# A two-layer hybrid decoder trunk: the last key tile in the ring of the others, memory banks read by halves together, and alternating rings for the second layer's key weights

## The chip and the metric

The kernel runs on one core of a Trainium2 chip. Its engines are named as the profile names them: PE (the matmul engine; PEld is its weight load), ACT, DVE, POOL and SP, which here only issues loads. The metric is the device time of one execution in microseconds (us), smaller being better; the median of three runs is given.

## The reference, cut to what matters

```python
mem_n = rmsnorm(mem, norm_mem)                    # 256 memory tokens
for layer in range(2):
    h = rmsnorm(x, norm_mix[layer])
    if layer == 0:                                # 8 heads x 64, strictly causal, and pooling
        q, k, v, u = split(h @ ab_w_in)
        mix = concat(stick_breaking_attention(q, k, v), multiscale_pool(u)) @ ab_w_out
    else:                                         # 64 groups of 16 channels, 64 complex states
        y = s5_ssm(h @ ssm_w_in)
        val, gate = split(gelu(y) @ ssm_w_glu)
        mix = val * sigmoid(gate)
    x = x + mix
    k, v = split(mem_n @ w_kv[layer])             # the keys and values of the memory
    x = x + cross_attention(rmsnorm(x, norm_xattn[layer]) @ w_q, k, v) @ w_o
    x = x + conv_gated_mlp(rmsnorm(x, norm_ffn[layer]))
return rmsnorm(x, norm_final)
```

There are 512 positions of 1024 channels, in fp32.

## The kernel before

Activations lie with channels on partitions, in tiles of 128 x 512. A product of two fp32 matrices is made of three matmuls on a high and a low part of each side (`mm3`, L206 to L209: high by high, high by low, low by high). The high part is a rounded copy made by ACT (`copy_hi`, L113), the low part the difference, made by DVE (`sub_lo`, L116).

Weights come as chunks of 128 x 512 through one stream, `W`. A chunk is loaded by SP into a raw buffer `wr`, and then split by ACT and DVE into a high and a low tile. A chunk of kind 0 goes to `wh` and `wl`, of which four pairs may wait ahead; one of kind 1 goes to `wth` and `wtl`, which are taken from the common ring of tiles `t` (`ttile`), and of those two pairs may wait ahead in the second layer. `W.take` hands PE the next chunk in the fixed order of the list and puts the splits of further chunks behind what ACT and DVE have been given so far. A chunk that is split late frees its raw buffer late, and SP waits for raw buffers.

Instructions run on each engine in the order in which the program is written: the two mixing stages are lists of small steps (`seq`), and each step gives each engine its part.

In the first layer's stage the steps of a head h are `z_(h)` (scores, PE `psz` at L1096 to L1103, then ACT and DVE), `f_(h)` (the running sums, PE at L1136, then the weights `swh` and `swl` by ACT and DVE) and `p_(h)` (weights times values, PE `pso`, split into `mh` and `ml`). `q_(p)` and `k_(p)` make the query and key tile of two heads: PE `psqk`, DVE `qkf`, then a split into `qk`. The tiles of pairs 0 to 2 lie in a ring `qk` of six buffers; those of pair 3 lie in the buffers `vh0` and `vh1` of the pool `kv0`, the home of the memory's values later on. The earlier tenant of `vh1` is `par`, parameters of the state-space stage; its last reader is PE's `psmu`.

Memory tokens enter by `acts(q)`: PE transposes two column blocks into one PSUM bank `psm` (L217), ACT writes the high part of each half (`mem`, L778), DVE the low part (L779). The banks of `psm`, `pso` and `psz` come from one rotation; the three banks of `z_(5)` are those that `acts(2)`, `p_(3)` and `acts(3)` have left, in this order (with the change `acts(2)`, `acts(3)`, `p_(3)`). `kk(m)` is PE's product of the memory with two key columns (`psk`), four chunks of 128 x 512.

In the second layer's stage the memory is transposed and scaled anew (`ac(q)`), between the steps of the state-space part. For a block b these are `um(b)` (PE `psu`, the input projection), `uo` and `sg` (out to DRAM and back in another layout, tile `sg`), `x1(b)` (PE `psX`; ACT `xs` and `mub`; DVE `sr`, `xs`, `sr` and the scan into `gg`), `x2(b)` (ACT `gsw`; DVE `gg`, `gsw` and `hb`) and `x3(b)` (PE `psY`, which needs `sg` and `hb`; ACT `sy`). `hb` is read from `psY`'s second matmul on (L1703).

Of the kernel before, what the change touches and what calls it, by code (L numbers as in the profile page):

```python
# [8 lines left out]
F32 = mybir.dt.float32  # L9
F32R = mybir.dt.float32r  # L10
I32 = mybir.dt.int32
BF16 = mybir.dt.bfloat16
AF = mybir.ActivationFunctionType
ALU = mybir.AluOpType
# [8 lines left out]
MEM = 256  # L23
# [29 lines left out]
def trunk_kernel(  # L53
# [12 lines left out]
    V, A, G, T = nc.vector, nc.scalar, nc.gpsimd, nc.tensor  # L66
# [28 lines left out]
    def psB(name="psB"):  # L95
        if "X" in pools:
            return psX(name)
        return pools["B"].tile([128, 512], F32, tag="ps", name=name)

    def psC(name="psC"):  # L100
        if "X" in pools:
            return psX(name)
        return pools["C"].tile([128, 512], F32, tag="ps", name=name)

    def ttile(name, dt=F32R):
        return tp.tile([128, 512], dt, tag="t", name=name)
# [5 lines left out]
    def copy_hi(o, i):  # L112
        A.activation(out=o, in_=i, func=AF.Copy)  # L113

    def sub_lo(o, i, hi):
        V.tensor_tensor(out=o, in0=i, in1=hi.bitcast(F32), op=ALU.subtract)  # L116
# [80 lines left out]
    def sproj(ps, acts, n=512, first=True, last=True):  # L197
        k, nk = 0, len(acts)
        while k < nk:
            hi, lo = W.take()  # L200
            for q in range(hi.shape[1]):
                mm3(ps, hi[:, q, :], lo[:, q, :], acts[k][0][:, :n], acts[k][1][:, :n],
                    first and k == 0, last and k == nk - 1)
                k += 1
# [11 lines left out]
    def tr(o, i, kk=128):  # L216
        T.transpose(o, i, ident[:kk, :kk])  # L217
# [14 lines left out]
    def gcol(idx, layer, m):  # L232
        c = goff[idx] + layer * KD + m
        return gcols[:, c:c + 1]
# [36 lines left out]
    def norm_row(rc, n, perm=False, dst=None, dg=None):  # L271
        if dg is None:
            dg = norm_diag(rc, n)
        pr = psC("psrow")
        T.matmul(pr[:, :n * 128], lhsT=ones, rhs=dg[:, :n, :], start=True, stop=True)
        if dst is None:
            dst = np_.tile([128, 512], F32, tag="rbc", bufs=1, name="rbc")
        if perm:
            A.activation(out=dst.rearrange("p (j k) -> p j k", j=8),
                         in_=pr.rearrange("p (k j) -> p j k", j=8), func=AF.Copy)  # L280
        else:
            A.activation(out=dst[:, :n * 128], in_=pr[:, :n * 128], func=AF.Copy)
        return dst
# [445 lines left out]
    class KV:  # L729
# [35 lines left out]
        def acts(self, m0=0, m1=KD):  # L765
            if m0 == 0:
                self.ma = []
            for m in range(m0, m1, 2):
                ps = psC("psm")
                for q in range(2):  # L770
                    for i in range(2):
                        tr(ps[:, q * MEM + i * 128:q * MEM + (i + 1) * 128],
                           self.mr[i][:, (m + q) * 128:(m + q + 1) * 128])
                for q in range(2):
                    t = ttile("mem")
                    h, l = t[:, 0:MEM], t[:, MEM:2 * MEM]
                    g, p = gcol(3, 0, m + q), ps[:, q * MEM:(q + 1) * MEM]
                    A.activation(out=h, in_=p, func=AF.Copy, scale=g)  # L778
                    V.scalar_tensor_tensor(out=l, in0=p, scalar=g, in1=h.bitcast(F32), op0=ALU.mult, op1=ALU.subtract)  # L779
                    self.ma.append((h, l))  # L780
            if m1 < KD:
                return
            self.kh = self.pool.tile([128, KD, MEM], F32R, tag="kh", name="kh")
            self.kl = self.pool.tile([128, KD, MEM], F32R, tag="kl", name="kl")
# [48 lines left out]
    def glu_col(i):  # L833
        return (i + 1) % 2 * KD + i // 2

    def ssm_weights():
        kw = KV.weights(1)
        for b in range(NB):
            W.cols(ssm_w_in[0], b)
            if b >= 4:  # L840
                W.todo += kw[4 * (b - 4):4 * (b - 3)]
        W.todo += kw[16:]
        for i in range(NG1):
            W.cols(ssm_w_glu[0], glu_col(i), 0, 6)
        for i in range(NG1):
            W.cols(ssm_w_glu[0], glu_col(i), 6, 2)
        for i in range(NG1, 2 * KD):
            W.cols(ssm_w_glu[0], glu_col(i))
# [22 lines left out]
    kv0 = tc.alloc_tile_pool(name="kv0", bufs=1, reuse_waits="tile")  # L871
# [16 lines left out]
    for q in ("kh", "kl"):  # L888
        t = kv0.tile([128, 2048], F32, tag=q, name="par")
        par += [t[:, c * 512:(c + 1) * 512] for c in range(4)]  # L890
    for q in ("vh0", "vh1"):
        t = kv0.tile([128, 1024], F32, tag=q, name="par")
# [148 lines left out]
    with region("rgA1") as rg, tc.manual_schedule():  # L1041

        def rt(tag, bufs, name, dt=F32):
            return rg.tile([128, 512], dt, tag=tag, bufs=bufs, name=name)

        vh, vl = [], []
        for i in range(4):
            h = rt("v", 8, "vh", F32R)
            l = rt("v", 8, "vl", F32R)
            A.activation(out=h, in_=pv[i], func=AF.Copy, scale=rcol0[:, i:i + 1])  # L1050
            V.scalar_tensor_tensor(out=l, in0=pv[i], scalar=rcol0[:, i:i + 1], in1=h.bitcast(F32),
                                   op0=ALU.mult, op1=ALU.subtract)
# [5 lines left out]
        def qk_tile(name, scale):  # L1058
            ps = psB("psqk")
            sproj(ps, n_mix0.acts)  # L1060
            if not rbc0:
                rbc0.append(norm_row(None, 4, dg=dg0))
            f = np_.tile([128, 512], F32, tag="ev", bufs=2, name="qkf")
            V.scalar_tensor_tensor(out=f, in0=ps, scalar=scale, in1=rbc0[0], op0=ALU.mult, op1=ALU.mult)
            if name[1] == 3:
                t = kv0.tile([128, 1024], F32R, tag="vh0" if name[0] == "q" else "vh1", name="qk3")
                h, l = t[:, 0:512], t[:, 512:1024]
            else:
                h, l = rt("qk", 6, "qkh", F32R), rt("qk", 6, "qkl", F32R)
            copy_hi(h, f)  # L1070
            sub_lo(l, f, h)
            qk[name] = (h, l)
# [140 lines left out]
        def seq(*fs):  # L1213
            for f in fs:
                if type(f) is int:
                    step(f)
                else:
                    f()
# [10 lines left out]
        q_ = lambda p: (lambda: qk_tile(("q", p), 0.125))  # L1229
        sq = lambda q: (lambda: kvm.square(q))  # L1230
        k_ = lambda p: (lambda: qk_tile(("k", p), 1.0))
        z_ = lambda h: (lambda: sb_z(h))
        f_ = lambda h: (lambda: sb_f(h))
        p_ = lambda h: (lambda: sb_p(h))
        u_ = lambda g: (lambda: pool_in(g))
        ud = lambda g: (lambda: pool_sum(g))
        uf = lambda g: (lambda: pool_fin(g))
        um = lambda g: (lambda: pool_mm(g))
        kk = lambda m: (lambda: kvm.k(m))
        acts = lambda q: (lambda: kvm.acts(2 * q, 2 * q + 2))  # L1240
# [2 lines left out]
        seq(f_(0), z_(1), k_(1), p_(0), 1, 1)  # L1243
        seq(f_(1), ud(2), z_(2), um(3), q_(2), uf(2), 1, p_(1), u_(1), um(2))
        seq(f_(2), kvm.stats, ud(1), z_(3), 1, u_(0), 1, uf(1), kvm.row, k_(2), 1, 1, 1, turn_on, p_(2))
        seq(f_(3), 1, um(1), 1, ud(0), 1, 1, q_(3), 1, z_(4), 1, 1, acts(0), acts(1), k_(3), 1, acts(2), p_(3), acts(3))
        seq(f_(4), fin, uf(0), z_(5), kk(0), p_(4), um(0), kk(1))
        seq(f_(5), z_(6), kk(2), p_(5), kk(3), v_(0))
        seq(f_(6), z_(7), v_(1), p_(6))
# [1 line left out]
        for m in range(KD):  # L1251
            ps = ab_out(m)
# [599 lines left out]
```

## Time and profile before

| | us |
|---|---|
| median of three runs | 1499.33 (1497.9 to 1500.23) |
| the profiled execution, its time | 1498.06 |
| its span, first to last instruction | 1496.3 |
| PE busy | 1477.7 (99%) |
| DVE busy | 1028.7 (69%) |
| ACT busy | 735.1 (49%) |
| POOL busy | 395.3 (26%) |

Page rows give the share of the whole span. The chain of work that ended last runs through PE for 92% of the span, DVE for 3%, ACT for 2%. The mean granted clock of PE is 0.994 of full speed. In a row of the trace in order of time, the bracket at the end gives how long the engine had been idle and what it had waited for; an operation with "x16" is a run of sixteen.

### The profile page before, as it was taken

Reading aid. Unit: us, or ns where it says so; the run is one execution under the profiler, and the core shown is the slowest. Engines: PE = TensorE matmul, PEld = TensorE weight load, DVE = VectorE, ACT = ScalarE, POOL = GpSimd, SP = SyncE. Lnnn points to the kernel's source line nnn. Section 1 sums busy time; section 2 is a strip of 40 time slices with the busy share of each in tenths; the row PEclk is TensorE's granted clock in tenths of the full one; section 3 lists DMA queues with packets and bytes.
Section 4 is the critical chain, followed back from the end, with each engine's and each line's share of the span. In section 5 each row is a group of like instructions: output and inputs, shape, how many; then the busy total and the mean of one; then the engine's idle time right before and its main releaser. Section 6 shows DMA issues by size and latency. Waiting matters only on the chain.

```text
span 1496.3 us, 21038 instructions
## 1 busy us (share of the span) xinstructions
PE 1477.7 (99%) x7347; PEld 1234.8 (83%) x7347; DVE 1028.7 (69%) x1607; ACT 735.1 (49%) x1304; POOL 395.3 (26%) x823
## 2 busy tenths in 40 slices
PE   8999999999999999999999999999999999999998
PEld 7887888888888887888788898888888888888887
DVE  4776776676688897888865766556567775377755
ACT  5566774344445534555664555434444543245533
POOL 7864119999000013333852120000000000000002
PEclk9999999999999999999999999999999999999999
DMA  6313243433433344444568985332233333333331
GB/s 183 98 46 102 67 151 100 119 94 104 129 99 107 113 147 147 123 123 132 158 189 302 269 269 182 106 97 67 60 94 89 97 97 97 100 95 99 97 115 57
DMA packets 271941, 183.99 MB, mean 123 GB/s; under 512 B 21271, under 2 KB 252763, under 8 KB 271835
## 3 DMA queue, kind: packets, MB, share of 16 engines
q1 hardware_dynamic: 244731, 132.79, 30.3%
q0 software_dynamic: 15872, 42.26, 8.5%
q10 hardware_dynamic: 11232, 7.61, 1.6%
q8 instruction: 57, 0.93, 0.3%
q14 instruction: 49, 0.40, 0.1%
HBM read 156.13 MB, written 24.12 MB: 120 GB/s over the span
## 4 chain that ended last, share of the span: by engine, by line
PE 92%; DVE 3%; ACT 2%; DMA 1%; issue 1%; SPq 0%; ACTq 0%; DVEq 0%; POOLq 0%; POOL 0%
PE psup L207 10%; PE psup L209 10%; PE psup L208 10%; PE psd L207 5%; PE psd L209 5%; PE psd L208 5%; PE pso L209 2%; PE pso L208 2%; PE pso L207 2%; PE psq L207 2%; PE psq L209 2%; PE psq L208 2%; PE psg L207 2%; PE psg L209 2%; PE psg L208 2%; PE psz L1136 1%
## 5 line engine op out<-in xcount | busy, mean ns | idle before, releaser
L116 DVE TENSOR_TENSOR wl<-wr,wh 128x512 fp32r<-128x512 f32 (+2 forms) x467 | 325.1, 713 | 143.9 <-ACT wh L113 142.8
L113 ACT ACTIVATE wh<-wr 128x512 fp32r<-128x512 f32 (+2 forms) x467 | 280.1, 617 | 249.5 <-PE psup L208 83.3
L207 PE MATMUL psup<-xh,wh 128*128 128x512 f32 x704 | 275.7, 392 | 0.0
L208 PE MATMUL psup<-xl,wh 128*128 128x512 f32 x704 | 274.4, 390 | 0.0
L209 PE MATMUL psup<-xh,wl 128*128 128x512 f32 x704 | 274.1, 389 | 0.0
L1542 POOL TENSOR_TENSOR acc<-acc,sq 128x256 f32<-128x256 f32 x12 | 8.8, 734 | 557.2 <-ACT sq L1540 557.0
L207 PEld LDWEIGHTS psup<-xh,wh 128*128 128x128 f32 x704 | 132.2, 188 | 28.5 <-issue 1.5
L209 PEld LDWEIGHTS psup<-xh,wl 128*128 128x128 f32 x704 | 132.2, 188 | 28.3 <-DVE wl L116 0.3
L208 PEld LDWEIGHTS psup<-xl,wh 128*128 128x128 f32 x704 | 132.2, 188 | 27.1 <-issue 0.2
L207 PE MATMUL psd<-hh,wh 128*128 128x512 f32 x328 | 130.5, 398 | 0.0
L209 PE MATMUL psd<-hh,wl 128*128 128x512 f32 x328 | 128.3, 391 | 0.0
L208 PE MATMUL psd<-hl,wh 128*128 128x512 f32 x328 | 127.9, 390 | 0.2 <-DVE hl L116 0.2
L1456 ACT ACTIVATE fc<-fu,ccols 128x512 f32<-128x512 f32 x44 | 36.0, 817 | 93.6 <-DVE fu L1454 93.6
L302 ACT ACTIVATE xh<-xT,gcols 128x512 fp32r<-128x512 f32 x40 | 33.4, 835 | 95.2 <-DVE xT L325 66.8
L207 PEld LDWEIGHTS psd<-hh,wh 128*128 128x128 f32 x328 | 61.6, 188 | 14.4 <-issue 1.5
L209 PEld LDWEIGHTS psd<-hh,wl 128*128 128x128 f32 x328 | 61.6, 188 | 13.6
L208 PEld LDWEIGHTS psd<-hl,wh 128*128 128x128 f32 x328 | 61.7, 188 | 13.0 <-DVE hl L116 0.5
L715 POOL DMA_DIRECT2D tz<-kt x128 | 65.1, 516 | 7.4 <-POOL kt L712 4.7
L303 DVE SCALAR_TENSOR_TENSOR xl<-xT,gcols,xh 128x512 fp32r<-128x512 f32 x40 | 35.2, 880 | 33.7 <-ACT xh L302 33.5
L207 PE MATMUL psq<-xh,wh 128*128 128x512 f32 x128 | 51.1, 400 | 0.0
L1401 DVE TENSOR_TENSOR fu<-psup,rbc 128x512 f32<-128x512 f32 x44 | 30.3, 688 | 29.2 <-PE psup L209 27.9
L207 PE MATMUL pso<-oh,wh 128*128 128x512 f32 x128 | 50.2, 392 | 0.0
(352 smaller groups left out, 3441.2 us busy)
## 6 DMA issues: line engine op xcount, KB each, us to landing
wr<-in_ffn_w_up_dram SPq DMA_DIRECT2D x176, 256.0 KB, 3.0
wr<-in_ffn_w_down_dram SPq DMA_DIRECT2D x70, 256.0 KB, 2.9
wr<-in_xa_w_kv_dram SPq DMA_DIRECT2D x64, 256.0 KB, 4.1
wr<-in_ab_w_in_dram SPq DMA_DIRECT2D x32, 256.0 KB, 2.8
wr<-in_xa_w_q_dram SPq DMA_DIRECT2D x32, 256.0 KB, 2.9
wr<-in_xa_w_o_dram SPq DMA_DIRECT2D x32, 256.0 KB, 2.8
wr<-in_ssm_w_glu_dram SPq DMA_DIRECT2D x29, 256.0 KB, 2.8
wr<-in_ffn_w_down_dram SPq DMA_DIRECT2D x24, 192.0 KB, 2.6
```

The costliest lines, as they stand in the source:

```text
L113: A.activation(out=o, in_=i, func=AF.Copy)
L116: V.tensor_tensor(out=o, in0=i, in1=hi.bitcast(F32), op=ALU.subtract)
L207: T.matmul(ps, lhsT=lh, rhs=rh, start=first, stop=False)
L208: T.matmul(ps, lhsT=lh, rhs=rl, start=False, stop=False)
L209: T.matmul(ps, lhsT=ll, rhs=rh, start=False, stop=last)
L302: A.activation(out=ho, in_=src, func=AF.Copy, scale=g)
L303: V.scalar_tensor_tensor(out=lo, in0=src, scalar=g, in1=ho.bitcast(F32), op0=ALU.mult, op1=ALU.subtract)
L715: nc.gpsimd.dma_start(out=tzs[b % 2][j:128:8, :, j * 16:128], in_=ktf[:, :, 0:128 - j * 16])
L1136: T.matmul(o_, lhsT=l_, rhs=r_, start=False, stop=(n_ == len(mms) - 1), skip_group_check=True)
L1401: V.tensor_tensor(out=u, in0=ps, in1=rbc, op=ALU.mult)
L1456: A.activation(out=c, in_=u, func=AF.Identity, scale=cwcol(layer, 2, t), bias=cbcol(layer, t))
L1542: G.tensor_tensor(out=acc[:, sl], in0=acc[:, sl], in1=sq[:, 0:256], op=ALU.add)
```

## The change

Four places in the code change.

- `KV.acts`: of a bank of two halves, ACT now reads both, and then DVE both. Before, the order was ACT, DVE, ACT, DVE, and each had to wait for the one ahead, since they read the same bank.
- `KV.weights(1, (0, 1))`: of the second layer's key chunks every second one is of kind 1, in the common ring (`wth`, `wtl`). The first layer has that already.
- `qk_tile`: the key tile of pair 3 takes the next two buffers of the ring `qk`, those of key tile 1, in place of `vh1`. The query tile of pair 3 stays in `vh0`.
- The list of the first layer: `acts(3)` stands ahead of `p_(3)`.

```diff
@@ -774,10 +774,12 @@
                 for q in range(2):
                     t = ttile("mem")
                     h, l = t[:, 0:MEM], t[:, MEM:2 * MEM]
-                    g, p = gcol(3, 0, m + q), ps[:, q * MEM:(q + 1) * MEM]
-                    A.activation(out=h, in_=p, func=AF.Copy, scale=g)
-                    V.scalar_tensor_tensor(out=l, in0=p, scalar=g, in1=h.bitcast(F32), op0=ALU.mult, op1=ALU.subtract)
+                    A.activation(out=h, in_=ps[:, q * MEM:(q + 1) * MEM], func=AF.Copy, scale=gcol(3, 0, m + q))
                     self.ma.append((h, l))
+                for q in range(2):
+                    h, l = self.ma[m + q]
+                    V.scalar_tensor_tensor(out=l, in0=ps[:, q * MEM:(q + 1) * MEM], scalar=gcol(3, 0, m + q),
+                                           in1=h.bitcast(F32), op0=ALU.mult, op1=ALU.subtract)
             if m1 < KD:
                 return
             self.kh = self.pool.tile([128, KD, MEM], F32R, tag="kh", name="kh")
@@ -834,7 +836,7 @@
         return (i + 1) % 2 * KD + i // 2
 
     def ssm_weights():
-        kw = KV.weights(1)
+        kw = KV.weights(1, (0, 1))
         for b in range(NB):
             W.cols(ssm_w_in[0], b)
             if b >= 4:
@@ -1062,8 +1064,8 @@
                 rbc0.append(norm_row(None, 4, dg=dg0))
             f = np_.tile([128, 512], F32, tag="ev", bufs=2, name="qkf")
             V.scalar_tensor_tensor(out=f, in0=ps, scalar=scale, in1=rbc0[0], op0=ALU.mult, op1=ALU.mult)
-            if name[1] == 3:
-                t = kv0.tile([128, 1024], F32R, tag="vh0" if name[0] == "q" else "vh1", name="qk3")
+            if name == ("q", 3):
+                t = kv0.tile([128, 1024], F32R, tag="vh0", name="qk3")
                 h, l = t[:, 0:512], t[:, 512:1024]
             else:
                 h, l = rt("qk", 6, "qkh", F32R), rt("qk", 6, "qkl", F32R)
@@ -1243,7 +1245,7 @@
         seq(f_(0), z_(1), k_(1), p_(0), 1, 1)
         seq(f_(1), ud(2), z_(2), um(3), q_(2), uf(2), 1, p_(1), u_(1), um(2))
         seq(f_(2), kvm.stats, ud(1), z_(3), 1, u_(0), 1, uf(1), kvm.row, k_(2), 1, 1, 1, turn_on, p_(2))
-        seq(f_(3), 1, um(1), 1, ud(0), 1, 1, q_(3), 1, z_(4), 1, 1, acts(0), acts(1), k_(3), 1, acts(2), p_(3), acts(3))
+        seq(f_(3), 1, um(1), 1, ud(0), 1, 1, q_(3), 1, z_(4), 1, 1, acts(0), acts(1), k_(3), 1, acts(2), acts(3), p_(3))
         seq(f_(4), fin, uf(0), z_(5), kk(0), p_(4), um(0), kk(1))
         seq(f_(5), z_(6), kk(2), p_(5), kk(3), v_(0))
         seq(f_(6), z_(7), v_(1), p_(6))
```

First place: ACT in the first layer, behind the weight splits, up to the scores' exponential. The names carry tile numbers; `psm` is the bank of one `acts`, `mh` the split of `pso`, and a bracket lists the engines that the instruction waits for. Before:

```order
L113 ACTIVATE qk3_1780<-qkf_1778 128x512 [waits DVE_49,PE_49,Pool_49]
L778 ACTIVATE mem_1797<-psm_1792,gcols_86 128x256
L778 ACTIVATE mem_1800<-psm_1792,gcols_86 128x256 [waits DVE_49]
L113 ACTIVATE mh_1519<-pso_1803 64x512
L778 ACTIVATE mem_1823<-psm_1818,gcols_86 128x256
L778 ACTIVATE mem_1826<-psm_1818,gcols_86 128x256 [waits DVE_49]
L1140 ACTIVATE psz_1644<-psz_1644 128x512
```

and after:

```order
L113 ACTIVATE qkh_1780<-qkf_1778 128x512 [waits DVE_49]
L777 ACTIVATE mem_1798<-psm_1793,gcols_86 128x256 [waits PE_49]
L777 ACTIVATE mem_1800<-psm_1793,gcols_86 128x256
L777 ACTIVATE mem_1809<-psm_1804,gcols_86 128x256 [waits PE_49]
L777 ACTIVATE mem_1811<-psm_1804,gcols_86 128x256
L113 ACTIVATE mh_1519<-pso_1817 64x512 [waits PE_49]
L1142 ACTIVATE psz_1644<-psz_1644 128x512 [waits PE_49]
```

What moved: the two `mem` of a bank no longer wait for DVE in between, the split of `pso` stands behind all four, and the copy of the key tile no longer waits for PE and POOL.

Second place: PE at the same point, as a piece of the difference (- is before, + after).

```order
 L217 MATMUL pssp<-cs,par 64x64 x8
-L217 MATMUL psm<-cs,mrow 128x128 x4
+L217 MATMUL psm<-cs,mrow 128x128 x8
 L207 MATMUL pso<-swh,vh 128x512
 L208 MATMUL pso<-swl,vh 128x512
```

The four transposes of `acts(3)`, which stood behind the twelve `pso` matmuls of `p_(3)`, now stand ahead of them.

Third place: ACT in the second layer, from the weight splits ahead of `x1(0)` to `x2(0)`. `xs` and `mub` belong to `x1(0)`, the four `mem` to `ac(1)` and `ac(2)`, and `gsw` to `x2(0)`. Before:

```order
L113 ACTIVATE wh_8547<-wr_8480 128x512 [waits DMAHW7_49,PE_49,Activation_49]
L1749 ACT_TABLE_LOAD
L1749 ACTIVATE gl_8573<-ones_77 128x4
L1673 ACTIVATE xs_8584<-psX_8575 64x512 [waits PE_49]
L1674 ACTIVATE xs_8584<-psX_8575 64x512
L1675 ACTIVATE mub_8342<-mu8_120 128x8x63
L778 ACTIVATE mem_8599<-psm_8594,gcols_86 128x256 [waits PE_49]
L778 ACTIVATE mem_8602<-psm_8594,gcols_86 128x256 [waits DVE_49]
L778 ACTIVATE mem_8610<-psm_8605,gcols_86 128x256 [waits PE_49]
L778 ACTIVATE mem_8613<-psm_8605,gcols_86 128x256 [waits DVE_49]
L1689 ACTIVATE gsw_8616<-gg_8592 64x512 [waits DMASW2_49]
```

and after:

```order
L113 ACTIVATE wh_8548<-wr_8481 128x512 [waits DMAHW7_49,PE_49,Activation_49]
L113 ACTIVATE wth_8554<-wr_8499 128x512 [waits DMAHW2_49]
L1751 ACT_TABLE_LOAD
L1751 ACTIVATE gl_8580<-ones_77 128x4
L1675 ACTIVATE xs_8591<-psX_8582 64x512 [waits PE_49]
L1676 ACTIVATE xs_8591<-psX_8582 64x512
L1677 ACTIVATE mub_8343<-mu8_120 128x8x63
L777 ACTIVATE mem_8606<-psm_8601,gcols_86 128x256 [waits PE_49]
L777 ACTIVATE mem_8608<-psm_8601,gcols_86 128x256
L777 ACTIVATE mem_8617<-psm_8612,gcols_86 128x256 [waits PE_49]
L777 ACTIVATE mem_8619<-psm_8612,gcols_86 128x256
L1691 ACTIVATE gsw_8623<-gg_8599 64x512 [waits DMASW2_49,DVE_49]
```

One more chunk is split here (`wth`, the second of the first `kk`), and the waits for DVE between the `mem` are gone. Further on, the two splits that stood behind `x1(1)` are three, and so the third and the fourth chunk of that `kk`, and the first of the next block, are split ahead of `x2(1)`; before, the fourth was split behind `x3(0)`'s output. DVE has the same changes in its own order. On POOL and SP the order is as it was.

## Rows read from the trace of the kernel before

**Rows 1.** Page, part 1: engine, busy us (share of the span), instructions.
```profile
PE 1477.7 (99%) x7347; PEld 1234.8 (83%) x7347; DVE 1028.7 (69%) x1607; ACT 735.1 (49%) x1304; POOL 395.3 (26%) x823
```

**Rows 2.** PE's waits: engine, line, waited for; us in total, times, longest.
```profile
PE psz L1096 <- DVE mem L779: 3.0, 1, 3.0
PE psY L1703 <- issue: 1.7, 1, 1.7
...
PE psk L209 <- DVE wl L116: 0.4, 1, 0.4
```

**Rows 3.** Windows: length; busy PE, PEld, DVE, ACT, POOL; clock; DMA share; GB/s.
```profile
152.00:153.00 1.00, 0.91 (x5) 0.65 (x5) 0.48 (x1) 0.97 (x3) 0.00 (x0) 0.50 0.00 0
```

**Rows 4.** The same windows, second place.
```profile
814.00:815.00 1.00, 1.00 (x7) 1.00 (x7) 0.48 (x1) 0.45 (x2) 0.54 (x2) 0.53 1.00 397
...
825.00:826.00 1.00, 0.50 (x2) 0.30 (x2) 1.00 (x2) 1.00 (x3) 0.94 (x2) 1.00 0.95 257
```

**Rows 5.** PE by time, first layer: start, us, operation, [idle before <-releaser].
```profile
150.45 0.41 PE L1096 MATMUL psz<-qkh 64*128 64x384 f32 x1 [3.01 <-DVE mem L779]
...
162.30 0.40 PE L207 MATMUL pso<-swh,vh 128*128 128x512 f32 x1
```

**Rows 6.** PE by time, undisturbed scores and the step behind.
```profile
130.60 0.44 PE L1096 MATMUL psz<-qkh 64*128 64x384 f32 x1
...
133.29 0.61 PE L217 MATMUL pssp<-cs,par 64*64 64x64 f32 x8
```

**Rows 7.** PE by time, undisturbed steps, second layer.
```profile
834.72 0.33 PE L1702 MATMUL psY<-sg,wq 128*128 128x64 f32 x2
...
838.21 0.36 PE L207 MATMUL psk<-mem,wh 128*128 128x256 f32 x1
...
844.05 1.89 PE L1671 MATMUL psX<-sg,wi 128*128 128x64 f32 x16
```

**Rows 8.** ACT in order of time, first layer.
```profile
140.81 0.84 ACT L778 ACTIVATE mem<-psm,gcols 128x256 fp32r<-128x256 f32 x2 [0.61 <-DVE mem L779]
142.29 0.47 ACT L778 ACTIVATE mem<-psm,gcols 128x256 fp32r<-128x256 f32 x1 [0.64 <-DVE mem L779]
...
147.53 0.63 ACT L113 ACTIVATE qk<-qkf 128x512 fp32r<-128x512 f32 x1 [2.69 <-PE psmu L217]
```

**Rows 9.** DVE in order of time, first layer.
```profile
145.73 0.69 DVE L1064 SCALAR_TENSOR_TENSOR qkf<-psqk,rbc 128x512 f32<-128x512 f32 x1
```

**Rows 10.** PE in order of time, second layer.
```profile
810.96 0.33 PE L1702 MATMUL psY<-sg,wq 128*128 128x64 f32 x2
812.99 0.41 PE L1703 MATMUL psY<-hb,wo 128*128 128x64 f32 x2 [1.69 <-issue]
...
825.20 0.39 PE L207 MATMUL psk<-mem,wh 128*128 128x256 f32 x1 [1.16 <-ACT wh L113]
...
827.44 1.90 PE L1671 MATMUL psX<-sg,wi 128*128 128x64 f32 x16
```

**Rows 11.** ACT in order of time, second layer.
```profile
804.32 0.46 ACT L778 ACTIVATE mem<-psm,gcols 128x256 fp32r<-128x256 f32 x1
807.64 0.84 ACT L778 ACTIVATE mem<-psm,gcols 128x256 fp32r<-128x256 f32 x2 [2.86 <-DVE mem L779]
...
809.55 0.63 ACT L1689 ACTIVATE gsw<-gg 64x512 f32<-64x512 f32 x1
...
817.16 1.13 ACT L113 ACTIVATE wh<-wr 128x512 fp32r<-128x512 f32 x2
```

**Rows 12.** DVE in order of time, second layer.
```profile
806.00 1.23 DVE L1681 TENSOR_TENSOR_SCAN gg<-mub,sr 128x512 f32<-128x512 f32 x1 [0.19 <-DVE sr L1679]
...
812.19 0.69 DVE L1693 TENSOR_TENSOR hb<-gg,gsw 128x512 f32<-128x512 f32 x1
```

**Rows 13.** Windows of 20 us behind the second place, columns as in rows 3.
```profile
840.00:860.00 20.00, 20.00 (x151) 19.02 (x150) 14.41 (x23) 10.39 (x18) 2.05 (x4) 1.00 0.92 263
```

**Rows 14.** The tile sg, 796 to 920 us: its loads' time to landing.
```profile
DMA to landing us min/median/max: 3.7/5.5/8.2
```

## The prediction

> **What bounds the kernel now.** I read the page first: PE is busy for 1477.7 of 1496.3 us [rows 1], so a change can gain only where PE stands idle (18.6 us in all) or runs at its lower clock. The list of PE's waits comes next. Its two largest single entries are the ones that this change touches: 3.0 us before `psz` in the first layer, 1.7 us before `psY` in the second; a small one, 0.4 us before `psk`, is a follower of the second place [rows 2]. Then the granted clock in windows of one microsecond: behind each of the two large waits, and nowhere else ahead of the last microseconds, it falls to 0.50, which is 1.2 in place of 2.4 GHz, for about six and a half microseconds [rows 3, 4]. So each of the two places costs twice: the wait, and the slow work behind it. Last, PE, ACT and DVE in order of time around both places tell which instruction is late and why [rows 5, 8 to 12]. DVE and ACT are far from full; what counts there is only when one instruction ends.
>
> **The first place (three of the four edits).** `z_(5)` starts at 150.45 after 3.01 us of idle time, and its scores and the `kk(0)` behind them end at 162.30 [rows 5]: 11.85 us. Undisturbed, the scores take 133.29 − 130.60 = 2.69 us [rows 6] and a `kk` 844.05 − 838.21 = 5.84 us [rows 7], together 8.53. So 3.32 us are lost to the clock there.
>
> Why is `z_(5)` late? It needs the bank of `acts(2)`, whose second low part DVE makes last. Ahead of it ACT stands still for 2.69 us before the copy of key tile 3, until `psmu` has left `vh1`, and starts at 147.53 [rows 8]. With the key tile in the ring that wait is gone (the slots' last tenant, key tile 1, was read by `z_(3)`, long before), and the copy starts when `qkf` is done. `qkf` ends now at 145.73 + 0.69 = 146.42 [rows 9]. The reading by halves takes from ACT the two waits for DVE of 0.61 and 0.64 us in `acts(0)` and `acts(1)` [rows 8]; the low parts start later in return, so I take 1.1 of these 1.25 us: `qkf` ends at 145.3. Behind it come the key copy (some 0.55), two high parts (0.42 each, from two in 0.84 [rows 8]) and two low parts of about that length: 145.4 + 0.55 + 0.84 + 0.9 = 147.7. PE has been idle since 150.45 − 3.01 = 147.44 [rows 5]. With `acts(3)` ahead of `p_(3)` the product `pso` waits a little longer for its turn on PE and for its bank, and I put PE's arrival 0.15 later, at 147.6. It would then start `z_(5)` at about 147.8: the start gains 2.66 us, with 0.2 of idle time left. For the other two banks `acts(3)` and `pso` are no later than the first; moving `acts(3)` forward is what makes the second one free, and by itself I give it nothing. The wait that is left is a tenth of the one behind which the clock fell, so I expect full speed: 3.32 more. **Sum 6.0 us**, with 2.7 as its lower end (the clock falls all the same) and 6.3 as its upper (no wait is left).
>
> **The second place (the reading by halves, and the alternating key weights).** From the start of `psY` at 810.96 to the end of `kk(0)` at 827.44 it takes 16.48 us [rows 10]; the same two steps one block later take 844.05 − 834.72 = 9.33 [rows 7]. Of the difference of 7.15, 1.69 is the wait for `hb`, 1.16 [rows 10] and 0.4 [rows 2] are waits for the splits of the fourth key chunk, and 3.9 is the clock, which is at half speed from 814 on [rows 4].
>
> `hb` starts at 812.19 [rows 12] since ACT's `gsw` starts only at 809.55, and that stands behind four `mem` of which the second waits 2.86 us for DVE [rows 11]: DVE has the scan to finish first, at 806.00 + 1.23 = 807.23 [rows 12]. With the halves together, ACT makes all four high parts from 804.32 to about 806, and `gsw` follows the scan's end at 807.3. DVE makes four low parts behind the scan (4 × 0.45, to 809.0) and then `gg`, `gsw` and `hb` (three of 0.69, to 811.1). PE asks for `hb` at 812.99 − 1.69 = 811.3 less the gap of the two instructions, some 811.1. So I expect a wait of 0 to 0.3 in place of 1.69.
>
> The key chunks: before, the third is split at 817.16 behind `mub` [rows 11], the fourth only behind `x3(0)`'s output, and PE waits for it at 825.20 [rows 10]. With a second ring the second chunk is split ahead of the four `mem`, so the third and fourth take the place at 817.16, which itself moves some 2.5 us forward with `hb`. PE would reach the third at about 810.96 + 3.49 + 2.9 = 817.4 (3.49 is 838.21 − 834.72 [rows 7], 2.9 half a `kk`), and its low part is ready about then: 0.3 us of new wait, from 0 to 1.2. What is queued behind the added split is DVE's work for `x1(0)`, which is still 1 us from its input, and ACT's table load, which has idle time behind it; SP gets a raw buffer sooner. The cost of the edit is nothing as long as that idle time covers one split. **Sum 7.15 − 0.3 = 6.85 us**, with 3 as the lower end (waits alone) and 7.15 as the upper.
>
> **What is late next.** Behind 827 PE waits for nothing for a long while (20.00 of 20.00 us busy at full clock), while the DMA engines are at 0.92 of their time [rows 13]. PE now comes 7 us earlier to loads that partly were issued independently of it, and one load of `sg` takes 3.7 to 8.2 us [rows 14]. The trace before can't show what that costs: between nothing, since each load is released by a step that also comes earlier, and the whole 6.85 us. I take 0.8, near the lower end, since [rows 13] shows the loop keeping pace at the rate it will have again.
>
> **Total: 6.0 + 6.85 − 0.8 = 12.0 us.** On the profiled execution that is 1498.06 − 12.0 = 1486.1; the median is 1.27 above that execution, so 1499.33 − 12.0 = 1487.3.
>
> **Rivals.**
> *The waits go, the clock falls all the same.* Then 2.66 + (1.69 + 1.56 − 0.3) = 5.6 us are gained: 1493.7. For it: at both places short waits may be left, next to small matmuls and transposes. Against it: at 825 PE is idle for half a microsecond of one, and its clock stays 1.00 [rows 4]; the same `psY` and `kk` without a wait run at full speed [rows 7].
> The Trainium skill ("TensorE: Matmul & The Clock Gate", section "A second HAM failure mode: psum-queue depth-cycling") says that short idle times between groups of matmuls, as banks change hands, can make PE's clock swing between its two levels. By that rule this rival's time would come out; the row at 825 speaks against it here.
>
> *The second place's gain is given back to the loads.* The first place stays, of the second 0 to 1.5 are kept: 1491.8 to 1493.3. For it: [rows 13, 14]; against it: the steps that issue the loads move along.
> The Trainium skill ("DMA: Bandwidth & Descriptors", "Specifications") gives about 358 GB/s as a core's limit from memory. The 263 GB/s of [rows 13] are under three quarters of that, and by that figure the stretch could be about a quarter shorter, so the gain would hold; no run here shows that limit.
>
> *The change doesn't do what it says.* `z_(5)` and `hb` each find another late input (the key's low part, `gsw` behind a DMA), and both waits and both slow stretches stay within 3 us of what they were: 1496.3 to 1499.3.
>
> *Slower.* In the blocks behind 827 `sg` lands after PE has come to `psX`, because PE is early and the DMA engines are at 0.92. Where such a wait is as long as the one before `psY`, it brings a slow stretch as well, 1.69 + 3.9 = 5.6 us. Three of them give back 16.8 of the 12.8: 1499.33 − 12.8 + 16.8 = 1503.3. It decides from three blocks on in which `sg` is more than 1.7 us late. Against it: no block before shows any such wait [rows 13].
>
> **Chances.** Forecast 0.66, clock 0.12, given back 0.10, no effect 0.07, slower 0.05. The forecast alone spans 1485.0 (all upper ends, less the spread of the runs) to 1491; with 0.66 in it, the range has to reach to the first two rivals, 1494.0. About 0.2% (3 us) is what a measurement of this kernel can tell from no change. Faster by more than that: 0.66 + 0.12 + 0.10 = 0.88; within it: 0.07; slower: 0.05.
>
> **What would show it.** Right: no wait over 0.5 us before `psz` at 148 or `psY` at 805, granted clock 1.00 through both, PE's idle total near 13 us. Each step has its row: the key copy right behind `qkf`, `gsw` at the scan's end, no wait for a key chunk over 0.5 us. Wrong: a low clock at either place, or new waits of PE before `psX`, `psu` or `psv` between 820 and 915, with `sg` or a weight split as what is waited for.

## The result, and the profile after

The changed kernel takes 1486.17 us (median of four executions, 1485.42 to 1491.18) against 1499.78 of the kernel before (1497.9 to 1500.61): a ratio of 0.9918, 95% interval 0.9901 to 0.9935. A second set of four, timed with the experiments, gave 1485.40 (1485.18 to 1486.25) and 0.9907 (0.9894 to 0.9919). The profiled execution took 1486.11 us, 11.95 less than the profiled one of before; its span is 1484.3 us at a mean granted clock of 0.998 (before 0.994).

PE's row of the page answers to [rows 1]:

```profile
PE 1471.6 (99%) x7347; PEld 1229.2 (83%) x7347; DVE 1026.6 (69%) x1607; ACT 733.1 (49%) x1304; POOL 396.6 (27%) x823
```

PE's idle time fell from 18.6 to 12.7 us (1484.3 − 1471.6), and its busy time by 6.1 us with the same number of instructions: that half of the gain is work done at the higher clock.

In the list of PE's waits (columns as in [rows 2]) the entries for `psY` and `psk` are gone, and that for `psz` is 0.2 us. The longest that is left stands at the start of the kernel, where the first weights arrive:

```profile
PE psv L207 <- ACT wh L113: 2.0, 2, 1.1
...
PE psz L1098 <- DVE mem L781: 0.2, 1, 0.2
```

The first place, PE in order of time; it answers to [rows 5, 6]:

```profile
148.38 0.41 PE L1098 MATMUL psz<-qkh 64*128 64x384 f32 x1 [0.21 <-DVE mem L781]
...
151.14 0.39 PE L207 MATMUL psk<-mem,wh 128*128 128x256 f32 x1
...
157.00 0.40 PE L207 MATMUL pso<-swh,vh 128*128 128x512 f32 x1
```

`psz` starts 0.21 us late in place of 3.01. From its start to the end of `kk(0)` it takes 157.00 − 148.38 = 8.62 us (before 11.85), in which the scores take 2.76 and the `kk` 5.86. ACT and then DVE at this place (before: [rows 8, 9]):

```profile
140.39 1.57 ACT L777 ACTIVATE mem<-psm,gcols 128x256 fp32r<-128x256 f32 x4 [0.40 <-ACT spo L511]
...
145.96 0.63 ACT L113 ACTIVATE qkh<-qkf 128x512 fp32r<-128x512 f32 x1 [1.93 <-DVE qkf L1066]
146.50 1.55 ACT L777 ACTIVATE mem<-psm,gcols 128x256 fp32r<-128x256 f32 x4
```

```profile
145.24 0.69 DVE L1066 SCALAR_TENSOR_TENSOR qkf<-psqk,rbc 128x512 f32<-128x512 f32 x1
...
147.36 1.66 DVE L781 SCALAR_TENSOR_TENSOR mem<-psm,gcols,mem 128x256 fp32r<-128x256 f32 x4
```

The reader sees the two edits at once: four `mem` in one run on each engine, where each had waited for the other, and the key copy (`qkh`) at 145.96, right behind `qkf` (145.24 + 0.69), where it had stood at 147.53 behind `psmu`.

The second place, PE, then ACT, then DVE (before: [rows 10 to 12]):

```profile
806.71 0.33 PE L1704 MATMUL psY<-sg,wq 128*128 128x64 f32 x2
806.88 0.39 PE L1705 MATMUL psY<-hb,wo 128*128 128x64 f32 x2
...
810.20 0.36 PE L207 MATMUL psk<-mem,wh 128*128 128x256 f32 x1
...
816.25 1.90 PE L1673 MATMUL psX<-sg,wi 128*128 128x64 f32 x16
```

```profile
800.07 1.55 ACT L777 ACTIVATE mem<-psm,gcols 128x256 fp32r<-128x256 f32 x4
803.01 0.63 ACT L1691 ACTIVATE gsw<-gg 64x512 f32<-64x512 f32 x1 [1.39 <-DVE gg L1683]
...
810.07 0.61 ACT L113 ACTIVATE wh<-wr 128x512 fp32r<-128x512 f32 x1
810.59 0.62 ACT L113 ACTIVATE wth<-wr 128x512 fp32r<-128x512 f32 x1
```

```profile
801.75 1.23 DVE L1683 TENSOR_TENSOR_SCAN gg<-mub,sr 128x512 f32<-128x512 f32 x1 [0.18 <-DMA wo<-d_wout]
802.89 1.64 DVE L781 SCALAR_TENSOR_TENSOR mem<-psm,gcols,mem 128x256 fp32r<-128x256 f32 x4
...
805.76 0.69 DVE L1695 TENSOR_TENSOR hb<-gg,gsw 128x512 f32<-128x512 f32 x1
```

`hb` ends at 806.45, and PE reads it at 806.88 without a wait. `psY` and the `kk(0)` behind it take 816.25 − 806.71 = 9.54 us, before 16.48. `gsw` starts at the end of the scan. The splits at 810.07 and 810.59 are the third and fourth key chunk.

The windows of both places (columns as in rows 3) show the higher clock throughout; the one stretch at 0.50 that is left starts at 1479.5 us, in the last microseconds (before at 1493.3):

```profile
148.00:150.00 2.00, 1.78 (x18) 1.44 (x16) 1.78 (x5) 1.92 (x5) 0.00 (x0) 1.00 0.39 117
150.00:152.00 2.00, 2.00 (x16) 1.48 (x14) 1.31 (x3) 1.94 (x5) 0.00 (x0) 1.00 0.00 0
806.00:808.00 2.00, 2.00 (x17) 1.85 (x15) 1.05 (x2) 0.54 (x2) 1.98 (x4) 1.00 1.01 397
808.00:810.00 2.00, 2.00 (x20) 2.00 (x20) 1.33 (x3) 1.94 (x4) 0.11 (x1) 1.00 0.98 350
```

### The profile page after: what moved, and what is told of

Its sections match the earlier page's. It is cut to its first block, busy times and chain, and to the rows that moved or that the text cites. A ratio compares the mean times of both kernels' runs of the same rounds, so it can differ in the third digit from the quotient of the medians.

```text
span 1484.3 us, 21038 instructions
## 1 busy us (share of the span) xinstructions
PE 1471.6 (99%) x7347; PEld 1229.2 (83%) x7347; DVE 1026.6 (69%) x1607; ACT 733.1 (49%) x1304; POOL 396.6 (27%) x823
## 4 chain that ended last, share of the span: by engine, by line
PE 94%; DVE 2%; ACT 1%; DMA 1%; issue 1%; SPq 0%; POOL 0%; POOLq 0%; ACTq 0%; DVEq 0%
PE psup L207 11%; PE psup L209 11%; PE psup L208 11%; PE psd L207 5%; PE psd L209 5%; PE psd L208 5%; PE pso L209 2%; PE pso L207 2%; PE pso L208 2%; PE psq L207 2%; PE psq L209 2%; PE psq L208 2%; PE psg L208 2%; PE psg L207 2%; PE psg L209 2%; PE psu L207 2%
## 5 line engine op out<-in xcount | busy, mean ns | idle before, releaser
L116 DVE TENSOR_TENSOR wl<-wr,wh 128x512 fp32r<-128x512 f32 (+2 forms) x459 | 319.9, 712 | 141.2 <-ACT wh L113 140.4
L113 ACT ACTIVATE wh<-wr 128x512 fp32r<-128x512 f32 (+2 forms) x459 | 275.6, 617 | 243.5 <-PE psup L208 83.4
L209 PEld LDWEIGHTS psd<-hh,wl 128*128 128x128 f32 x328 | 61.6, 188 | 13.6
```

The costliest lines, as they stand in the source:

```text
L209: T.matmul(ps, lhsT=ll, rhs=rh, start=False, stop=last)
```

## The experiments

Each is the changed kernel or the kernel before with one edit, timed beside the kernel before on one chip. n is the number of executions.

| run | median us (lowest to highest), n | ratio to before, 95% interval |
|---|---|---|
| no_halves | 1494.06 (1493.09 to 1494.82), 4 | 0.9960, 0.9945 to 0.9975 |
| no_alt | 1493.87 (1491.94 to 1496.30), 5 | 0.9963, 0.9950 to 0.9976 |
| no_key | 1493.95 (1491.51 to 1496.48), 4 | 0.9954, 0.9938 to 0.9971 |
| no_order | 1487.82 (1485.66 to 1489.80), 4 | 0.9919, 0.9904 to 0.9933 |
| only_halves | 1497.26 (1493.94 to 1500.07), 10 | 0.9984, 0.9975 to 0.9992 |
| only_alt | 1497.10 (1495.75 to 1500.30), 10 | 0.9982, 0.9973 to 0.9992 |
| only_key | 1497.96 (1496.64 to 1500.35), 10 | 0.9994, 0.9984 to 1.0003 |
| hb_late2 | 1487.58 (1487.06 to 1488.10), 2 | 0.9920, 0.9902 to 0.9938 |
| hb_late3 | 1490.26 (1490.23 to 1490.28), 2 | 0.9938, 0.9921 to 0.9955 |
| after_again | 1485.40 (1485.18 to 1486.25), 4 | 0.9907, 0.9894 to 0.9919 |
| sg_early | 1485.61 (1485.11 to 1494.93), 6 | 0.9930, 0.9907 to 0.9953 |
| sg_mid | 1486.18 (1485.27 to 1494.93), 6 | 0.9922, 0.9904 to 0.9941 |

### One edit taken back: no_halves, no_alt, no_key, no_order

The theory is the prediction's: each place costs its wait and the slow clock behind it, and an edit pays where its wait is the last one at its place. The rivals say that one edit carries a place and the others trim it.

**no_halves** takes the reading by halves back:

```diff
-                    A.activation(out=h, in_=ps[:, q * MEM:(q + 1) * MEM], func=AF.Copy, scale=gcol(3, 0, m + q))
+                    g, p = gcol(3, 0, m + q), ps[:, q * MEM:(q + 1) * MEM]
+                    A.activation(out=h, in_=p, func=AF.Copy, scale=g)
+                    V.scalar_tensor_tensor(out=l, in0=p, scalar=g, in1=h.bitcast(F32), op0=ALU.mult, op1=ALU.subtract)
                     self.ma.append((h, l))
-                for q in range(2):
-                    h, l = self.ma[m + q]
-                    V.scalar_tensor_tensor(out=l, in0=ps[:, q * MEM:(q + 1) * MEM], scalar=gcol(3, 0, m + q),
-                                           in1=h.bitcast(F32), op0=ALU.mult, op1=ALU.subtract)
```

> The changed kernel, but each memory bank is read half by half in turn again (ACT, DVE, ACT, DVE). Theory (each place costs its wait and, behind a wait of about 1.7 us or more, some 3.3 us of slow clock): in the first layer the key copy starts near 146.5, the second low part of acts(2) ends 2.8 us later as before, PE waits about 1.8 us before psz and the clock falls; in the second layer hb is late by 1.7 us again and the clock falls there too, only the wait for the fourth key chunk is gone. About 1496 to 1498 us, both slow stretches back. Rival (the key tile's ring and the alternating weights are what count, the order of reading is worth only its own waits of 1.25 us and 1.7 us): 1489 to 1490, clock 1.00 at both places.

Measured: 1494.06, some 8 us of the gain lost, more than the rival says and less than the theory. The second place is as the theory has it (1.7 us before `psY`, clock 0.50 from 813 to 820; against the changed kernel 4.8 us lost there). The first place is not: PE does not wait before `psz`, it waits earlier, in front of `psm` and `pso`, which now stand behind two banks read half by half. PE in order of time, and two windows:

```profile
142.32 0.66 PE L217 MATMUL psm<-cs,mrow 128*128 128x128 f32 x4 [0.33 <-DVE mem L779]
143.80 0.56 PE L207 MATMUL pso<-swh,vh 128*128 128x512 f32 x1 [0.82 <-DVE mem L779]
```

```profile
143.00:144.00 1.00, 0.20 (x1) 0.20 (x2) 0.71 (x2) 1.00 (x3) 0.00 (x0) 1.00 0.00 0
...
145.00:146.00 1.00, 1.00 (x5) 0.98 (x4) 1.00 (x3) 0.31 (x1) 0.00 (x0) 0.50 0.36 104
```

These 1.1 us of waits brought a slow stretch of some 3.4 us (144 to 147.5), half as long as before, and the place lost 2.3 us by the end of `kk(0)`, where about 5 was expected (1.8 in place of 0.2 of wait, and the clock).

**no_alt** is `kw = KV.weights(1)` again.

> The changed kernel, but all key chunks of the second layer go through one ring again. Theory: the first layer is as in the changed kernel; hb is on time, so psY runs at full speed and PE comes to the fourth key chunk at about 3.5 us before its split, a longer wait than any left, behind which the clock falls: the edit that alone would be worth 1.6 us is worth 3.5 to 7 here; 1490 to 1493 us. Rival (the alternation is worth only the 1.6 us that PE waited for the chunk before): 1487.8.

Measured: 1493.87. The lost 8 us are more than either said. PE in order of time at `kk(0)`, and a window behind it:

```profile
813.47 0.39 PE L209 MATMUL psk<-mem,wl 128*128 128x256 f32 x1 [1.40 <-DVE wl L116]
...
818.05 0.39 PE L207 MATMUL psk<-mem,wh 128*128 128x256 f32 x1 [1.70 <-ACT wh L113]
...
819.00 0.39 PE L209 MATMUL psk<-mem,wl 128*128 128x256 f32 x1 [0.45 <-DVE wl L116]
```

```profile
822.00:824.00 2.00, 2.00 (x11) 2.00 (x11) 1.92 (x3) 0.63 (x1) 0.00 (x0) 0.50 1.03 408
```

The wait is 3.55 us in sum, as the theory had it (3.5), split over the third and the fourth chunk, and the clock falls behind it from 819 to 827; the two together cost 7.8 us on the way from `psk` to the end of the stage. An edit that removed 1.6 us of waits in the kernel before is worth 8 once `hb` is on time. The profiled execution holds one more slow stretch, from 85.8 to 89.2 us, far from the edit and behind no wait: PE is busy ahead of it.

```profile
82.00:84.00 2.00, 1.98 (x16) 1.52 (x14) 1.28 (x2) 1.97 (x4) 1.84 (x3) 1.00 0.45 131
...
86.00:88.00 2.00, 2.00 (x4) 0.87 (x4) 1.94 (x4) 0.03 (x1) 1.94 (x5) 0.50 0.00 0
```

It is not part of the 7.8 us: at 212 us this execution stands level with the changed kernel.

**no_key** puts the key tile back in `vh1`:

```diff
-            if name == ("q", 3):
-                t = kv0.tile([128, 1024], F32R, tag="vh0", name="qk3")
+            if name[1] == 3:
+                t = kv0.tile([128, 1024], F32R, tag="vh0" if name[0] == "q" else "vh1", name="qk3")
```

> The changed kernel, but the last key tile lies in vh1 again. Theory: its copy waits for psmu until about 148, and psz starts 2.3 to 2.5 us after PE is free, behind which the clock falls: 5 to 6 us lost, 1491 to 1492.5; the second layer as in the changed kernel. Rival (DVE's and ACT's own load of weight splits is what makes psz late, and the tile's place is worth under 1 us): 1486.5 to 1487.

Measured: 1493.95, 1.5 us above the theory's upper end. The list of PE's waits names what was expected, 2.5 us before `psz`, with the clock at 0.50 from 151 to 158 behind it, and a second one that was not:

```profile
PE psX L1673 <- DMA sg<-d_u: 2.9, 1, 2.9
PE psz L1098 <- DVE mem L781: 2.5, 1, 2.5
```

The second one is the last `psX` of the state-space stage, which waits for the load of `sg`. PE at that point, and a window behind it:

```profile
894.87 2.84 PE L1673 MATMUL psX<-sg,wi 128*128 128x64 f32 x16 [2.94 <-DMA sg<-d_u]
```

```profile
900.00:901.00 1.00, 1.00 (x3) 0.73 (x3) 0.95 (x2) 0.62 (x2) 0.00 (x0) 0.50 0.90 320
```

This is the mechanism of the prediction's rival "slower", once instead of three times: with the clock at 0.50 behind it (896 to 903) it costs 6.4 us in this execution. The other executions of this kernel are 2 to 5 us shorter, so it need not stand in each of them. The first place alone lost 5.3 us at the end of `kk(0)` (2.3 at the start of `psz`), of which 1.1 came back by 212 us.

**no_order** puts `p_(3)` ahead of `acts(3)` again.

> The changed kernel, but p_(3) stands ahead of acts(3) again. Theory: nothing is lost, since psz starts when the bank of acts(2) is free, and its other two banks are free by the time PE comes to them, 1.2 and 1.8 us later: 1485.5 to 1487. Rival (the move is what frees the second and third bank in time): the low parts of acts(3) come last on DVE and psz's third bank waits 0.5 to 1.5 us, and the clock may fall: 1487.5 to 1491.

Measured: 1487.82, in the rival's range; by the times alone the interval can't tell it from the changed kernel. The trace can. PE in order of time at the first place, and at the second `kk` of the second layer; then a window behind each:

```profile
147.52 0.41 PE L1098 MATMUL psz<-qkh 64*128 64x384 f32 x1 [0.57 <-DVE mem L781]
...
833.86 0.39 PE L209 MATMUL psk<-mem,wtl 128*128 128x256 f32 x1 [2.29 <-DVE wtl L116]
```

```profile
150.00:151.00 1.00, 1.00 (x5) 0.56 (x4) 0.31 (x2) 0.97 (x3) 0.00 (x0) 0.50 0.00 0
```

```profile
834.00:835.00 1.00, 1.00 (x9) 1.00 (x10) 1.00 (x2) 0.00 (x0) 0.00 (x0) 1.00 0.88 328
```

The banks are free in time, as the theory says: there is no wait at `psz`'s second or third bank. But PE comes to `psz` earlier, since four transposes fewer stand in front, waits 0.57 us in place of 0.21, and the clock falls for some 3.4 us behind it. The place loses 1.5 us by the end of `kk(0)`, of which 1.1 come back by 212 us, as in no_key. So the move has a worth, and it is neither the theory's nothing nor the rival's banks: it puts PE's own work where PE would have waited. The 2.29 us at 833.86 belong to a key chunk whose load was late in this execution; behind them the clock stayed at 1.00.

### One edit alone: only_halves, only_alt, only_key

> The kernel before with the reading by halves alone. Theory: in the first layer the key copy still waits for psmu, PE waits about 2.4 us before psz and the clock falls; the gain there is 0.5 us. In the second layer psY is on time, but PE then comes 3 us or more too early to the fourth key chunk; the gain there is 3.5 us at most, and it may be nothing if the clock falls behind that wait. 1495 to 1499. Rival (the reading by halves is the change, the others trim): 1488 to 1491.

> The kernel before with the alternating key weights alone. Theory (an edit pays only where its wait is the last one at its place): hb is as late as before and the clock falls behind it, only the 1.6 us that PE waited for the fourth key chunk go: 1497 to 1498. Rival (the alternation also lets the loads run earlier through the whole stage): 1492 to 1495.

> The kernel before with the last key tile in the ring alone. Theory: the key copy starts 1.0 us earlier, behind qkf; psz starts 1.0 us earlier, behind a wait of 2 us, and the clock falls as before: 1498 to 1499. Rival (the tile's place is what set the first place): 1493 to 1495, full clock there.

Measured: 2.0, 2.6 and 1.8 us below the kernel before in the medians, all near the theory's ranges, none near the rivals'; only_key's interval holds no change. In only_alt the two large waits stand as they were (PE's waits):

```profile
PE psz L1096 <- DVE mem L779: 3.3, 2, 3.0
PE psY L1703 <- issue: 1.7, 1, 1.7
```

In only_key `psz` still waits 1.92 us; against the same earlier point it starts 1.1 us sooner than before, as expected. What was not expected: the clock falls only from 153.0 to 156.4, half as long as before, and another 1.1 us are gained there. At the second place the wait before `psY` is the same (1.70 us), but the clock stays at 0.50 from 811.8 to 822.0, 10.2 us in place of 6.8; PE then comes to the fourth key chunk later and waits 0.3 us for it in place of 1.6, so that the place takes as long as before. PE at the first place, and a window at each:

```profile
150.01 0.41 PE L1096 MATMUL psz<-qkh 64*128 64x384 f32 x1 [1.92 <-DVE mem L779]
```

```profile
154.00:156.00 2.00, 2.00 (x10) 2.00 (x11) 1.33 (x4) 1.67 (x4) 0.00 (x0) 0.50 0.00 0
...
820.00:822.00 2.00, 2.00 (x11) 2.00 (x11) 0.29 (x2) 1.38 (x3) 0.00 (x0) 0.50 0.99 317
```

In only_halves PE's waits are 2.5 us before `psz`, and 1.7 and 1.8 before `psk`, where PE now comes too early. The three edits alone sum up to 6.4 us, the whole change gives 13.6; taking back any one of the three costs about 8.

### The price of one wait: hb_late3, hb_late2

The changed kernel, with idle subtractions on DVE in front of `hb`'s products; three, and then two:

```diff
             A.activation(out=gsw[64:128], in_=gg[0:64], func=AF.Copy)
+            for _ in range(3 if b == 0 else 0):
+                V.tensor_tensor(out=hbs[0][:, :, 1:65], in0=gg.rearrange("p (g k) -> p g k", g=8),
+                                in1=gsw.rearrange("p (g k) -> p g k", g=8), op=ALU.subtract)
             V.tensor_tensor(out=gg, in0=gg, in1=tb[:, 0, :], op=ALU.mult)
```

> The changed kernel with three idle subtractions on DVE (0.69 us each, into the tile that hb overwrites) ahead of x2(0)'s products, so that hb comes 2.1 us later and PE waits about 1.7 us before psY, as before the change; all else as in the changed kernel. Theory (the wait and the slow clock are one price): clock 0.50 for some 6.5 us behind it, and 1.7 + 3.3 to 3.9 lost: 1491 to 1492. Rival (the slow clock came from the waits for key chunks or from the crowded loads as well): clock 1.00, 1487.9.

> As hb_late3 with two idle subtractions, so that PE waits about 1.0 us before psY. Theory (the clock stays behind a wait that short): 1486.2 to 1487, that is 1.0 more than the changed kernel, clock 1.00. Rival (the clock falls behind any wait here): 1489 to 1490.

hb_late3, PE in order of time and a window behind it:

```profile
808.05 0.41 PE L1708 MATMUL psY<-hb,wo 128*128 128x64 f32 x2 [1.69 <-issue]
```

```profile
810.00:811.00 1.00, 1.00 (x6) 1.00 (x6) 0.70 (x2) 0.99 (x2) 0.00 (x0) 0.50 1.00 360
```

The wait is 1.69 us, to the hundredth that of before, and the clock is at 0.50 behind it, from 809 to 816. The time is 1490.26, 0.7 below the theory's range and 2.4 above the rival's time. It is 4.9 above the changed kernel beside it: 1.7 for the wait and 3.2 for the clock. hb_late2:

```profile
808.52 0.41 PE L1708 MATMUL psY<-hb,wo 128*128 128x64 f32 x2 [0.97 <-issue]
```

```profile
810.00:811.00 1.00, 1.00 (x12) 1.00 (x11) 0.70 (x2) 0.96 (x3) 0.09 (x1) 1.00 1.05 385
```

The wait is 0.97 us, the clock stays at 1.00, and from `psY` to the next `psX` 1.5 us are lost, 1.0 in the wait and 0.3 in one at `psk`. The median of 1487.58 is above the expected 1487: the profiled execution of 1488.10 has one more slow stretch at 86 to 90 us, far from the edit, behind a wait of 0.55 us. Behind one of 0.50 at the same instruction the clock stayed at 1.00 (after_again, only_key).

```profile
83.20 0.44 PE L1098 MATMUL psz<-qkh 64*128 64x384 f32 x1 [0.55 <-ACT qkh L113]
```

The two runs differ in 0.7 us of DVE work and in 3.4 us between `psY` and the next `psX` at the same place, with the loads and key chunks as in the changed kernel. So at this place the slow clock is not from the loads: the longer wait brings it. That is one trace of each; the executions without a trace (1490.23 and 1487.06) agree with it.

### What was late next: after_again, sg_early, sg_mid

> The changed kernel once more, as the base for the run beside it. Theory (the slack of the last load of sg has shrunk from 3.8 us to 0.5, so that in some executions PE waits for it and the clock falls behind): most runs 1485.4 to 1487, one in four or five at 1489 to 1492 with a mean clock lower by 0.002 to 0.003. Rival (the long run seen once was a disturbance from outside): all runs within 1485 to 1487.5.

Measured: all four executions within 1485.18 and 1486.25, as the rival has it. With the four of the result that is one long execution in eight, too few to decide.

sg_early and sg_mid change the order of POOL's loads in one step of the second layer's list. sg_early:

```diff
-            seq(kk(3), x1(5), ly(5), vs_(0), x2(5), x3(4), ly(6), lx(7), sg(7), yl(4), x4(1), vs_(1))
+            seq(kk(3), x1(5), ly(5), vs_(0), x2(5), x3(4), sg(7), lx(7), ly(6), yl(4), x4(1), vs_(1))
```

> The changed kernel, with one edit: the last load of sg is issued ahead of the loads for x1(7) and x3(6) instead of behind them (about 2 us earlier, and ahead of 2 MB in its queue). Theory: it lands some 5 us earlier, psX of block 7 waits for nothing, and the runs draw together at 1485 to 1486.5; median 0 to 1 us below the changed kernel, no run above 1488. Rival 1 (the long runs have another cause): no change in the spread. Rival 2 (wi, which psX needs as well, or wq and wo are then what is late): 1487 to 1491, the wait is at the same psX or at the psY behind it.

sg_mid:

```diff
-            seq(kk(3), x1(5), ly(5), vs_(0), x2(5), x3(4), ly(6), lx(7), sg(7), yl(4), x4(1), vs_(1))
+            seq(kk(3), x1(5), ly(5), vs_(0), x2(5), x3(4), sg(7), ly(6), lx(7), yl(4), x4(1), vs_(1))
```

> As sg_early, but the loads for x3(6) stay ahead of those for x1(7), and only the load of sg moves to their front. Theory (the two executions of sg_early at 1494 to 1495 came from wq and wo for x3(6), which stood last there): no execution above 1488, median 1485.2 to 1486. Rival (they came from other loads that are late in some executions, which neither order touches): one or two of six executions above 1489 again.

In the changed kernel the longest load of `sg` takes 10.8 us (before 8.2, [rows 14]):

```profile
DMA to landing us min/median/max: 3.7/5.4/10.8
```

It is the last one, issued at 876.5; it lands at 887.3, and `psX` takes it up at 887.8, 0.5 us later (before 3.8). In sg_early it lands 7.9 us ahead of its use. Yet the medians are the same, and the long executions have not gone: two of six are at 1494 to 1495 with sg_early, two of six at 1489 to 1495 with sg_mid, one of eight at 1491.18 with the changed kernel. None of them was the profiled one. So the theory that the load of `sg` makes them is not borne out, and the one on `wq` and `wo` isn't either; what does is open. Their mean clock is lower by 0.002 to 0.004, about what one or two slow stretches of 6.8 us would take from it. In sg_mid the slack moved rather than grew: the load of `wi` for the same `psX` lands at 887.2, 0.1 us ahead of its use (3.1 in the changed kernel), so a late `wi` stays possible there. Neither order is better than the changed kernel.

## Why the prediction was right

The forecast was 1487.3 in 1485 to 1494; 1486.17 was measured. Point by point, from the two profiled executions, by the starts of the same PE instruction in both:

| stretch | predicted gain us | measured |
|---|---|---|
| start of the kernel, to 21 us | 0 | −0.7 |
| first place, to the end of `kk(0)` | 6.0 | 6.0 |
| behind it, to 212 us | 0 | −1.1 |
| second place, to the end of `kk(0)` | 6.85 | 6.9 |
| behind it | −0.8 | +0.8 |
| sum, by the times | 12.0 | 11.95 |

The two places came out within 0.1 us each. That the sums agree to 0.05 is luck: two terms of the table that were put at nothing lost 1.8 us together, the last one missed by 1.6 the other way, and by the medians the gain is 13.6.

**The first place.** The wait left before `psz` was put at 0.2 and is 0.21; the key copy was put at 145.4 and came at 145.96, since the whole execution ran 0.66 us later from its first weights on. The clock stayed up, as forecast. The one step that failed is a small one: the moved `acts(3)` was given nothing, for the reason that the banks were free. They were, but no_order showed that it is worth some 1.5 us at this place (0.35 by 212 us), by filling PE's wait. The reason given for full speed, that the wait left is a tenth of the one behind which the clock fell, is weaker than it looks: the clock fell behind 0.57 us in no_order.

**The second place.** `hb` was expected at 811.1 on the clock of before, ended at 806.45, 4.25 us of which are the gain so far, so 810.7. The new wait at the third chunk, put at 0.3, shows as 0.16 us of PE's weight load, behind `wl` at 813.51. Of the 3.9 us that the prediction gave to the clock, hb_late3 shows 3.2 for the same wait; in the kernel before, half speed for the 6.8 us from 814.1 to 820.9 makes 3.4.

**What is late next.** This term (0.8) had the right sign and a fitting size, but the wrong place, so it was right by chance. Behind the second place nothing was given back in the profiled execution; a wait of 0.47 us before `psv` at 892 went away besides. The DMA engines now show a share of 1.05 over 810 to 840, where the prediction leaned on 0.92, and PE is busy all the time (columns as in rows 3):

```profile
810.00:820.00 10.00, 10.00 (x77) 9.49 (x77) 7.73 (x12) 4.21 (x8) 1.44 (x3) 1.00 1.05 386
820.00:840.00 20.00, 20.00 (x137) 18.43 (x136) 12.84 (x19) 9.76 (x16) 3.53 (x6) 1.00 1.05 317
```

The 386 GB/s over ten microseconds are above the 358 that the Trainium skill ("DMA: Bandwidth & Descriptors", "Specifications") gives as a core's limit from memory. The loop's traffic also holds writes to and reads from DRAM buffers of the kernel; the measurement decides, and the figure was no bound for the sum. What was given back lies in the first layer, between 185 and 212 us, in waits mostly too small for PE's list; PE's weight loads show two of them, behind a weight split on DVE and behind POOL:

```profile
PEld psv L208 <- DVE wtl L116: 0.6, 1, 0.6
PEld psz L1138 <- POOL spl L1119: 0.5, 1, 0.5
```

There, too, PE has come earlier to work whose time had not moved; no_key and no_order, in which it comes later again, got the same 1.1 us back between the first place and 212 us.

**The rivals.** "The waits go, the clock falls all the same" was wrong for the change, and what spoke against it (a wait of half a microsecond without a fall) is borne out at `psY` by hb_late2 (0.97 us) and bounded by no_order and by the 0.55 us of hb_late2 at 83 us, which did bring short falls. The Trainium skill ("TensorE: Matmul & The Clock Gate", "A second HAM failure mode: psum-queue depth-cycling") tells of a kernel whose clock swings as PE idles shortly between groups of matmuls in each round through the banks. The nearest cases here are no_halves and no_order, with two waits and with one as banks change hands, and a clock that falls for 3.4 us. "Slower" has its mechanism in the trace of no_key, once, at 6.4 us; the slack of the last `sg` shrank to 0.5 us, so the rival was nearer than its 0.05 would suggest, though three such waits were never seen.

## What to carry to other kernels

Where PE is the bound, read a wait together with the granted clock behind it: here two waits of 4.7 us in sum carried some 7 us of slow work with them, and shortening one by a third (only_key, 3.0 to 1.9 us) left half of its slow stretch there. Edits at one place should be costed as a chain: each of three edits was worth about 2 us alone and 8 us as the last one missing. When PE is made to come earlier, list the next inputs in order of time and their slack, since a slack that shrinks from 3.8 to 0.5 us shows in no median.

## What the runs showed of the hardware that was not expected

- The length of one wait doesn't decide alone whether the clock falls. It fell behind 1.69 us (before, hb_late3), behind 0.57 us (no_order) and behind 0.33 and 0.82 us near each other (no_halves), and it stayed at 1.00 behind 0.97 us (hb_late2) and behind 2.29 us (no_order, at 834). In no_alt it fell at 85.8 us with PE busy for 7.98 of the 8 us from 78 to 86. What decides is not shown.
- Slow stretches ahead of the last microseconds lasted some 3.4 us (no_halves, no_order), some 6.8 us (before, hb_late3) and once 10.2 us (only_key), the last two behind the same wait of 1.7 us before `psY`.
- With the DMA engines at a share of 1.00, a load of `sg` of 256 KB took 10.8 us (12.8 at 0.94 in no_key), against 3.7 at a share of 0.75 at the least in the same stage.
